# Unread products at the start, later input squares, and a shorter last norm in a two-layer decoder trunk

## The chip, the cores and the metric

The kernel runs on one core of one Trainium2 chip. The metric is the device time of one execution in microseconds (us). Lower is better.

## What is computed

The input is 256 tokens of width 2048, and everything is float32. There are two residual layers. The first has a gated token mixer, the second an attention with forget gates, and each is followed by a feed-forward part with a width-3 causal convolution. Every part begins with an RMS norm, and one more stands at the end. The weights are read once: 417.9 MB. Cut to what matters here:

```
def rmsnorm(x, g):
    r = lax.rsqrt(jnp.mean(x * x, axis=-1, keepdims=True) + EPS)
    return x * r * g

h = x
z = gelu(rmsnorm(h, a_norm) @ a_w_in)          # 2048 -> 4096, halves u and v
h = h + (u * mix(rmsnorm(v, a_v_norm))) @ a_w_out
h = h + conv_ffn(rmsnorm(h, f_norm[0]))        # up 2048 -> 11264, down 5632 -> 2048
h = h + attention(rmsnorm(h, b_norm), keys and values from h)
h = h + conv_ffn(rmsnorm(h, f_norm[1]))        # its down product is the last product of all
return rmsnorm(h, final_norm)
```

## The kernel before

The residual stream `h` lies in SBUF with the feature on the partition: 16 feature tiles of 128, each 256 tokens wide. It is the input, loaded in eight pieces of two tiles (`load_input`), that grows into the output.

**Two parts for every operand.** A product is made to nearly float32 accuracy out of three products in a shorter format. Each weight piece `raw` is split into `whi` (ScalarE, L82) and `wlo`, the rest (VectorE, L83). Each activation tile in the same way: `X[:, kt, :256]` is the rounded part (ScalarE, L221), `X[:, kt, 256:]` the rest (VectorE, L222). TensorE multiplies hi by hi, lo by hi and hi by lo, all on L166.

**The stream.** `Stream` sets the order of all work. Every weight matrix is cut into pieces of 128 x 1024 (512 KB). At step i the program issues the load of piece i + 6 (SyncE queue), the split of piece i + 3, the products of piece i, and then lets every pending generator run up to its next `yield` (`advance`). There are four `raw` buffers and four pairs of `whi` and `wlo`. So a load waits for the split that frees its buffer, and a split waits for the products that free its pair.

**The start.** The first 32 pieces are the v half of `a_w_in`, in four blocks (`tok_block`); activations are the stationary operand there, weights the moving one with 512 columns. A piece of it is 12 products. For the first block each piece also needs its own two tiles of `h`: `input_prep` splits them, has ScalarE square them, and has GpSimd add the squares into `acc` (`square_into_acc(c - 1, nc.gpsimd)`, L266 to L271). The first piece is cut into two halves. I number the pieces of this block 1 to 8.

**Norms.** The scale of each token is applied after the product. `token_sums` sums `acc` over the partitions with TensorE (L244, one moving column of ones, float32) and makes the inverse root on VectorE: a first guess from the bits (L232) and three Newton rounds of three small instructions (L234 to L236). `token_rows` turns the two columns of scales into rows on TensorE (L254). `v_done` reads a v block out of PSUM with Gelu and the scale; a block fills one of three PSUM tiles `ps`.

**The end.** The last down product has eight output blocks of two feature tiles (`feat_block`, 11 pieces each). Weights are stationary. `whi` multiplies 512 columns, the rounded half and the rest of `ffn_H` side by side, and `wlo` multiplies 256, so two halves of `ps` must be added to `h`: L300 and L301 for each tile in `final`. Then follow the squares, for the eighth block (p = 7) the norm, and four multiplications with four output loads (L314, L316).

Of the kernel before, what the change touches and what calls it, by code (L numbers as in the profile page):

```python
# [17 lines left out]
P = 128  # L18
D = 2048
T = 256  # L20
# [112 lines left out]
def build(ctx, tc, d, out):  # L133
# [31 lines left out]
    def mm(o, a, b, start, stop):  # L165
        nc.tensor.matmul(o, a, b, start=start, stop=stop, skip_group_check=True)  # L166

    def feat_block(src, x, K, done):

        box = {}  # L170
        n = K // 4
        for c in range(n):
            def mult(hi, lo, c=c):
                if c == 0:
                    box["ps"] = main_ps()
                ps, xx = box["ps"], x()
                parts = (hi, lo) if c < n - 1 else (lo, hi)
                for i, part in enumerate(parts):
                    for j in range(4):
                        kt = 4 * c + j  # L180
                        for m in range(2):
                            w = part[:, j * 256 + m * P:j * 256 + (m + 1) * P]
                            if part is hi:
                                mm(ps[:, m, :], w, xx[:, kt, :], kt == 0, kt == K - 1)
                            else:
                                mm(ps[:, m, :T], w, xx[:, kt, :T], False, False)
                if c == n - 1:
                    s.start(done(ps))
            s.chunk(src[c], mult)
# [39 lines left out]
    def rsqrt(y, v, n):  # L229

        t = small.tile([P, n], F32, name="rs_t", tag=f"rs_t{n}", bufs=2)
        nc.vector.tensor_scalar(y.bitcast(I32), v.bitcast(I32), -0.5, 1597463007.0, op0=OP.mult, op1=OP.add)  # L232
        for _ in range(3):
            nc.vector.scalar_tensor_tensor(t, y, -0.5, y, op0=OP.mult, op1=OP.mult)  # L234
            nc.vector.tensor_tensor(t, t, v, op=OP.mult)
            nc.vector.scalar_tensor_tensor(y, t, 1.5, y, op0=OP.add, op1=OP.mult)  # L236

    def token_sums(rest=None):

        mp = misc_ps()  # L240
        parts = [acc] + ([] if rest is None else [rest[:, 0, :], rest[:, 1, :]])
        for tb in range(2):
            for i, a in enumerate(parts):
                nc.tensor.matmul(mp[:, tb:tb + 1], a[:, tb * P:(tb + 1) * P], ones[:, :1],  # L244
                                 start=i == 0, stop=i == len(parts) - 1)
        v = small.tile([P, 2], F32, name="ts_v", tag="ts_v", bufs=2)
        nc.vector.tensor_scalar(v, mp[:, :2], 1.0 / D, EPS, op0=OP.mult, op1=OP.add)
        rsqrt(rcol, v, 2)
# [12 lines left out]
        yield  # L261
        nc.scalar.activation(rB, token_rows()[:, :T], AF.Copy)

    def square_into_acc(p, eng=nc.vector):
        sq = small.tile([P, 2, T], F32, name="sq", tag="sq", bufs=2)
        nc.scalar.activation(sq, h[:, 2 * p:2 * p + 2, :], AF.Square)  # L266
        if p == 0:
            eng.tensor_tensor(acc, sq[:, 0, :], sq[:, 1, :], op=OP.add)
        else:
            for i in range(2):  # L270
                eng.tensor_tensor(acc, acc, sq[:, i, :], op=OP.add)  # L271

    def scaled_sum(ps, a):

# [5 lines left out]
    def residual(p, gain):  # L280
# [10 lines left out]
                yield from token_scale()  # L291
        return done

    def final(p, gain):

        def done(ps):
            kts = (2 * p, 2 * p + 1)
            sq = small.tile([P, 2, T], F32, name="sq", tag="sq", bufs=2)
            for m, kt in enumerate(kts):
                nc.vector.tensor_tensor(h[:, kt, :], h[:, kt, :], ps[:, m, :T], op=OP.add)  # L300
                nc.vector.tensor_tensor(h[:, kt, :], h[:, kt, :], ps[:, m, T:], op=OP.add)  # L301
                nc.scalar.activation(sq[:, m, :], h[:, kt, :], AF.Square)
            for kt in kts:
                nc.scalar.activation(h[:, kt, :], h[:, kt, :], AF.Copy, scale=column(gain + kt))
            if p == 0:
                nc.vector.tensor_tensor(acc, sq[:, 0, :], sq[:, 1, :], op=OP.add)
            elif p < 7:
                for i in range(2):
                    nc.vector.tensor_tensor(acc, acc, sq[:, i, :], op=OP.add)
            else:  # L310
                token_sums(sq)
                mp = token_rows()
                for a, b in ((0, 2), (2, 6), (6, 11), (11, 16)):
                    nc.vector.tensor_tensor(h[:, a:b, :], h[:, a:b, :],  # L314
                                            mp[:, None, :T].to_broadcast([P, b - a, T]), op=OP.mult)
                    nc.sync.dma_start(out[:, a:b, :], h[:, a:b, :])  # L316
            yield
        return done
# [37 lines left out]

    def v_done(blk):
        def done(ps):
            _, vt, _, _, ss = mlp_kept()
            for tb in range(2):  # L360
                vv = vt[:, tb, blk * 512:(blk + 1) * 512]
                nc.scalar.activation(vv, ps[:, tb, :], AF.Gelu, scale=rcol[:, tb:tb + 1])
                sq = small.tile([P, 2, T], F32, name="sq", tag="sq", bufs=2)
                nc.scalar.activation(sq.rearrange("p a b -> p (a b)"), vv, AF.Square,
                                     accum_out=ss[:, tb, blk:blk + 1])
# [230 lines left out]
    def g_done(p):  # L596
        def done(ps):
# [4 lines left out]
            while state["done"] < NH or state["gates"] < p:  # L602
# [6 lines left out]
        return done  # L609


    state = {"layer": 0, "heads": [], "done": 0, "gates": 0}
    cd = dram.tile([NH, T], F32, name="cd")

    nc.scalar.dma_start(col[:, :C_KVNORM], d["col"][:, :C_KVNORM])
# [4 lines left out]
    nc.gpsimd.memset(ident, 1.0)  # L620
    nc.gpsimd.affine_select(ident, ident, pattern=[[-1, P]], compare_op=OP.is_equal, fill=0.0,
                            base=0, channel_multiplier=1)
    input_prep(0)

    for blk in range(4):
# [88 lines left out]
```

## Time and profile before

| | before |
|---|---|
| median of 3 runs | 2249.75 us (2249.28 to 2250.73) |
| the profiled execution | 2249.42 us |
| its span, first to last instruction | 2247.7 us |
| TensorE (PE) busy | 2227.7 us, 99% |
| weight load (PEld) | 1920.1 us, 85% |
| VectorE (DVE) | 1530.0 us, 68% |
| ScalarE (ACT) | 1190.9 us, 53% |
| GpSimd (POOL) | 34.7 us, 2% |
| read from HBM | 417.88 MB, 187 GB/s over the span |

The profile covers one execution. Times in its rows are microseconds from the span's start, and a row of the timeline gives start, length, engine, line, operation, output<-inputs and a count; in brackets stands idle time of the engine ahead of it and what ended it. Starts of successive products tell TensorE's pace better than their lengths, since products overlap in the pipeline.

### The profile page before, as it was taken

The numbers are of one execution on the slowest core, as the hardware profiler recorded it, in microseconds if no ns is written. First come the engines' busy times: TensorE is split into PE (matmuls) and PEld (weight loads), VectorE is DVE, ScalarE is ACT, GpSimd is POOL, SyncE is SP. The second block draws the span as 40 slices with busy tenths as digits, with TensorE's granted clock in tenths as the row PEclk, the third lists the DMA queues.
The fourth block names the chain that finished last, engine by engine and source line by source line (L and its number), as shares of the span: only waits on it lengthen the run. The fifth ranks groups of instructions, "written<-read, shape, count | busy, mean of one in ns | idle before, by whom it ended". The sixth has DMA issues, their size and how long they took to land.

```text
span 2247.7 us, 32221 instructions
## 1 busy us (share of the span) xinstructions
PE 2227.7 (99%) x12440; PEld 1920.1 (85%) x12440; DVE 1530.0 (68%) x2212; ACT 1190.9 (53%) x1622; POOL 34.7 (2%) x56
## 2 busy tenths in 40 slices
PE   8999999999999999999999999999999999999997
PEld 6888888888888888888788888888888888888886
DVE  6576677777777755557786567677777777765554
ACT  6544455555555544445444666446555555554442
POOL 3000000000000000000000110000000000000000
PEclk9999999999999999999999999999999999999998
DMA  7565555555555655555555555555555556555553
GB/s 281 186 189 172 191 191 192 189 189 194 190 190 190 191 181 193 197 188 177 171 185 188 167 164 185 181 197 188 189 191 192 189 192 191 190 185 197 189 192 116
DMA packets 116442, 422.11 MB, mean 188 GB/s; under 512 B 13232, under 2 KB 13376, under 8 KB 116032
## 3 DMA queue, kind: packets, MB, share of 16 engines
q1 hardware_dynamic: 115344, 417.93, 56.7%
q0 software_dynamic: 768, 2.10, 0.4%
q8 instruction: 97, 1.59, 0.3%
q14 instruction: 57, 0.47, 0.1%
q10 hardware_dynamic: 176, 0.02, 0.0%
HBM read 417.88 MB, written 2.11 MB: 187 GB/s over the span
## 4 chain that ended last, share of the span: by engine, by line
PE 98%; DVE 1%; ACT 0%; DMA 0%; issue 0%; SPq 0%; DVEq 0%
PE ps L166 96%; PE mp L388 0%; PE mp L472 0%; PE mp L558 0%; DMA raw<-a_in_v 0%; PE mp L573 0%; DVE wlo L83 0%; PE mp L581 0%; PE mp L582 0%; PE mp L557 0%; PE mp L580 0%; DVE X L222 0%; DVE h L314 0%; PE mp L244 0%; ACT whi L82 0%
## 5 line engine op out<-in xcount | busy, mean ns | idle before, releaser
L83 DVE TENSOR_TENSOR wlo<-raw,whi 128x1024 fp32r<-128x1024 f32 (+1 forms) x786 | 954.1, 1222 | 381.5 <-ACT whi L82 380.1
L82 ACT ACTIVATE whi<-raw 128x1024 fp32r<-128x1024 f32 (+1 forms) x786 | 821.8, 1054 | 383.7 <-PE ps L166 346.7
L166 PE MATMUL ps<-X,whi 128*128 128x512 f32 x3328 | 829.6, 396 | 0.0
L166 PEld LDWEIGHTS ps<-X,whi 128*128 128x128 f32 x3328 | 602.3, 188 | 120.7
L166 PEld LDWEIGHTS ps<-X,wlo 128*128 128x128 f32 x3328 | 426.0, 188 | 28.3
L166 PE MATMUL ps<-X,wlo 128*128 128x256 f32 x3328 | 430.7, 277 | 0.0
L166 PE MATMUL ps<-ffn_H,whi 128*128 128x512 f32 x1408 | 354.0, 395 | 0.0
L166 PEld LDWEIGHTS ps<-ffn_H,whi 128*128 128x128 f32 x1408 | 252.7, 188 | 48.5
L276 ACT ACTIVATE half<-ps 128x512 f32<-128x512 f32 x104 | 62.3, 599 | 256.0 <-PE ps L166 256.0
L166 PEld LDWEIGHTS ps<-ffn_H,wlo 128*128 128x128 f32 x1408 | 184.3, 188 | 14.5
L166 PE MATMUL ps<-ffn_H,wlo 128*128 128x256 f32 x1408 | 186.4, 277 | 0.0
L277 DVE TENSOR_TENSOR ffn_a<-ps,half 128x512 f32<-128x512 f32 x88 | 60.9, 692 | 175.3 <-ACT half L276 175.3
L166 PE MATMUL ps<-whi,X 128*128 128x512 f32 x512 | 163.6, 397 | 5.8 <-ACT whi L82 5.8
L166 PE MATMUL ps<-whi,att_X 128*128 128x512 f32 x512 | 168.0, 400 | 0.0
L422 DVE SCALAR_TENSOR_TENSOR ffn_c<-ffn_a,col,ffn_c 128x255 f32<-128x255 f32 x352 | 162.0, 481 | 6.3
L418 ACT ACTIVATE ffn_c<-ffn_a,col 128x256 f32<-128x256 f32 x176 | 96.4, 595 | 47.3 <-DVE ffn_a L278 47.3
L166 PEld LDWEIGHTS ps<-whi,X 128*128 128x128 f32 x512 | 97.0, 189 | 26.3 <-ACT whi L82 5.8
L166 PEld LDWEIGHTS ps<-whi,att_X 128*128 128x128 f32 x512 | 96.2, 188 | 20.5
L166 PE MATMUL ps<-wlo,X 128*128 128x512 f32 x256 | 100.9, 394 | 1.3 <-DVE wlo L83 1.3
L166 PE MATMUL ps<-wlo,att_X 128*128 128x512 f32 x256 | 100.1, 391 | 0.0
L221 ACT ACTIVATE X<-h,col 128x256 fp32r<-128x256 f32 x64 | 29.0, 500 | 101.8 <-DVE h L285 99.5
L226 ACT ACTIVATE ffn_H<-ffn_c 128x256 fp32r<-128x256 f32 x88 | 36.8, 418 | 70.0 <-DVE ffn_c L426 70.0
(140 smaller groups left out, 1223.4 us busy)
## 6 DMA issues: line engine op xcount, KB each, us to landing
raw<-up SPq DMA_DIRECT2D x352, 512.0 KB, 3.7
raw<-down SPq DMA_DIRECT2D x176, 512.0 KB, 3.9
raw<-a_in_u SPq DMA_DIRECT2D x32, 512.0 KB, 3.5
raw<-a_out SPq DMA_DIRECT2D x32, 512.0 KB, 3.9
raw<-b_q SPq DMA_DIRECT2D x32, 512.0 KB, 4.2
raw<-kvf_k SPq DMA_DIRECT2D x32, 512.0 KB, 3.5
raw<-kvf_v SPq DMA_DIRECT2D x32, 512.0 KB, 3.8
raw<-b_g SPq DMA_DIRECT2D x32, 512.0 KB, 3.3
```

What stands on the lines that cost most here:

```text
L82: self.nc.scalar.activation(hi[:, :n], raw, AF.Copy)
L83: self.nc.vector.tensor_tensor(lo[:, :n], raw, hi[:, :n].bitcast(F32), op=OP.subtract)
L166: nc.tensor.matmul(o, a, b, start=start, stop=stop, skip_group_check=True)
L221: nc.scalar.activation(dst[:, kt, :T], h[:, kt, :], AF.Copy, scale=g)
L226: nc.scalar.activation(dst[..., :T], src, AF.Copy)
L276: nc.scalar.activation(t, ps[:, :, T:], AF.Copy)
L277: nc.vector.tensor_tensor(a, ps[:, :, :T], t, op=OP.add)
L418: nc.scalar.activation(c[:, m, :], a[:, m, :], AF.Identity, scale=w[2], bias=column(C_CONVB + l * 2 * KF + f))
L422: nc.vector.scalar_tensor_tensor(c[:, m, n:], a[:, m, :T - n], w[k], c[:, m, n:], op0=OP.mult, op1=OP.add)
```

## The change

It has four parts.

1. `warm_up(9)`: nine 128 x 128 float32 products of the identity with itself into a PSUM tile that nobody reads, ahead of the first real product.
2. The squares of the input leave GpSimd. `input_prep` no longer squares; `input_norm` waits three steps and then squares one pair of tiles in each of eight steps, ScalarE squaring and VectorE adding. The sums, the scales and `rB` come after that, and `v_done` waits until `state["normed"]` is set.
3. In the last output block (`last_block`, p = 7) each feature tile gets its own run of 12 products of 256 columns in each piece, all into one 256-column half of `ps`. So one addition to `h` is enough for a tile, and tile 14 is added and squared while the products of tile 15 run (`final_tile`). The sums of `acc` go ahead of the products of tile 15 in the last piece.
4. In the last norm ScalarE takes the square root, VectorE its reciprocal, and one Newton round follows instead of a guess and three. A tiny Sqrt at p = 5 brings the table load forward.

```diff
+    def last_block(src, x, K, done, last):
...
+                for m in range(2):
+                    for part, half in ((lo, 0), (hi, 1), (hi, 0)):
+                        for j in range(4):
+                            kt = 4 * c + j
+                            mm(ps[:, m, :T], part[:, j * 256 + m * P:j * 256 + (m + 1) * P],
+                               xx[:, kt, half * T:(half + 1) * T], part is lo and kt == 0,
+                               half == 0 and part is hi and kt == K - 1)
+                    if c == n - 1:
+                        last(ps, m)
...
+    def newton(y, v, t):
+        nc.vector.scalar_tensor_tensor(t, y, -0.5, y, op0=OP.mult, op1=OP.mult)
+        nc.vector.tensor_tensor(t, t, v, op=OP.mult)
+        nc.vector.scalar_tensor_tensor(y, t, 1.5, y, op0=OP.add, op1=OP.mult)
...
+    def final_tile(ps, m):
+
+        kt = KD - 2 + m
+        if m == 0:
+            tail["sums"] = misc_ps()
+            tail["sq"] = small.tile([P, 2, T], F32, name="sq", tag="sq", bufs=2)
+            sum_tokens(tail["sums"], acc, True, False)
+        nc.vector.tensor_tensor(h[:, kt, :], h[:, kt, :], ps[:, m, :T], op=OP.add)
+        nc.scalar.activation(tail["sq"][:, m, :], h[:, kt, :], AF.Square)
+
+    def sum_tokens(mp, a, first, last):
+        for tb in range(2):
+            nc.tensor.matmul(mp[:, tb:tb + 1], a[:, tb * P:(tb + 1) * P], ones[:, :1],
+                             start=first and tb == 0, stop=last and tb == 1, skip_group_check=True)
...
             for kt in kts:
                 nc.scalar.activation(h[:, kt, :], h[:, kt, :], AF.Copy, scale=column(gain + kt))
...
-                token_sums(sq)
+            if p == 5:
+                nc.scalar.activation(warm, ones, AF.Sqrt)
+            if p == 7:
+                for m in range(2):
+                    sum_tokens(tail["sums"], tail["sq"][:, m, :], False, m == 1)
+                v = small.tile([P, 2], F32, name="ts_v", tag="ts_v", bufs=2)
+                nc.vector.tensor_scalar(v, tail["sums"][:, :2], 1.0 / D, EPS, op0=OP.mult, op1=OP.add)
+                t = small.tile([P, 2], F32, name="rs_t", tag="rs_t2", bufs=2)
+                nc.scalar.activation(t, v, AF.Sqrt)
+                nc.vector.reciprocal(rcol, t)
+                newton(rcol, v, t)
                 mp = token_rows()
...
     def input_prep(c):
         for kt in (2 * c, 2 * c + 1):
             prep(X1, kt, C_ANORM)
-        if c >= 1:
-            square_into_acc(c - 1, nc.gpsimd)
         if c == 7:
             s.start(input_norm())
 
+    def warm_up(n):
+
+        mp = misc_ps()
+        for _ in range(n):
+            nc.tensor.matmul(mp[:, :P], ident, ident, start=True, stop=True)
+
     def input_norm():
-        square_into_acc(7, nc.gpsimd)
-        yield
+        for _ in range(3):
+            yield
+        for p in range(8):
+            yield
+            square_into_acc(p)
         yield
         token_sums()
         yield
         nc.scalar.activation(rB, token_rows()[:, :T], AF.Copy)
+        state["normed"] = True
...
     def v_done(blk):
         def done(ps):
+            while not state["normed"]:
+                yield
...
-            feat_block(d[f"down{l}"][11 * p:11 * p + 11], ffn_h, KF, done(p))
+            feat_block(d[f"down{l}"][11 * p:11 * p + 11], ffn_h, KF, done(p), final_tile if l and p == 7 else None)
...
+    warm_up(9)
     input_prep(0)
```

How it moves instructions is seen at three places. Each row is a line of the program, an operation, output<-inputs, the shape and a count; line numbers are those of the kernel that the rows belong to. The first place is VectorE (DVE) at the start, from piece 7 of the first block on; `X_73` is the split input, `wlo` a weight piece's rest, `acc` the sum of squares. Before:

```order
L83 TENSOR_TENSOR wlo<-raw,whi 128x1024
L222 SCALAR_TENSOR_TENSOR X_73<-h,col,X_73 128x256 x2
L83 TENSOR_TENSOR wlo<-raw,whi 128x1024 x2
L247 TENSOR_SCALAR ts_v<-mp 128x2
L232 TENSOR_SCALAR rcol<-ts_v 128x2
```

After, at the same place on VectorE:

```order
L83 TENSOR_TENSOR wlo<-raw,whi 128x1024
L246 SCALAR_TENSOR_TENSOR X_73<-h,col,X_73 128x256 x2
L83 TENSOR_TENSOR wlo<-raw,whi 128x1024 x5
L291 TENSOR_TENSOR acc<-sq 128x256
L83 TENSOR_TENSOR wlo<-raw,whi 128x1024
L294 TENSOR_TENSOR acc<-acc,sq 128x256 x2
```

The additions, which stood on GpSimd, now lie between the weight splits of the second and third block, two to a piece; ahead of them VectorE's order in the first block is what it was.

The second place is TensorE (PE) at the end of the program; `sq` holds the squares of the last two tiles. Before:

```order
L166 MATMUL ps<-ffn_H,wlo 128x256 x16
L166 MATMUL ps<-ffn_H,whi 128x512 x8
L244 MATMUL mp<-ones,acc 128x1
L244 MATMUL mp<-ones,sq 128x1 x2
L244 MATMUL mp<-ones,acc 128x1
L244 MATMUL mp<-ones,sq 128x1 x2
L254 MATMUL mp<-ident,rcol 128x128 x2
```

After, TensorE's last rows:

```order
L166 MATMUL ps<-ffn_H,wlo 128x256 x4
L166 MATMUL ps<-ffn_H,whi 128x256 x8
L329 MATMUL mp<-ones,acc 128x1 x2
L166 MATMUL ps<-ffn_H,wlo 128x256 x4
L166 MATMUL ps<-ffn_H,whi 128x256 x8
L329 MATMUL mp<-ones,sq 128x1 x4
L277 MATMUL mp<-ident,rcol 128x128 x2
```

The two sums of `acc` have moved into the last piece, and the four sums of `sq` are alone behind it, the first two of them over tile 14.

The third place is VectorE at the end, from the last weight split on. Before, up to the end of the first Newton round (L234 to L236 come twice more, and then L314):

```order
L83 TENSOR_TENSOR wlo<-raw,whi 128x1024 x8
L300 TENSOR_TENSOR h<-h,ps 128x256
L301 TENSOR_TENSOR h<-h,ps 128x256
L300 TENSOR_TENSOR h<-h,ps 128x256
L301 TENSOR_TENSOR h<-h,ps 128x256
L247 TENSOR_SCALAR ts_v<-mp 128x2
L232 TENSOR_SCALAR rcol<-ts_v 128x2
L234 SCALAR_TENSOR_TENSOR rs_t<-rcol 128x2
L235 TENSOR_TENSOR rs_t<-rs_t,ts_v 128x2
L236 SCALAR_TENSOR_TENSOR rcol<-rs_t,rcol 128x2
```

After, up to the first output multiplication:

```order
L83 TENSOR_TENSOR wlo<-raw,whi 128x1024 x8
L324 TENSOR_TENSOR h<-h,ps 128x256 x2
L355 TENSOR_SCALAR ts_v<-mp 128x2
L358 RECIPROCAL rcol<-rs_t 128x2
L261 SCALAR_TENSOR_TENSOR rs_t<-rcol 128x2
L262 TENSOR_TENSOR rs_t<-rs_t,ts_v 128x2
L263 SCALAR_TENSOR_TENSOR rcol<-rs_t,rcol 128x2
L362 TENSOR_TENSOR h<-h,mp 128x512
```

Two of four additions are gone, and of ten small instructions between `ts_v` and the scales four are left, with a square root of ScalarE between `ts_v` and the reciprocal.

More of the change, by code (lines that the diff above doesn't have):

```diff
@@ L166, in mm, with feat_block @@
         nc.tensor.matmul(o, a, b, start=start, stop=stop, skip_group_check=True)
-    def feat_block(src, x, K, done):
+    def feat_block(src, x, K, done, last=None):
+        if last:
+            return last_block(src, x, K, done, last)
         box = {}
@@ L186, in mult @@
                                 mm(ps[:, m, :T], w, xx[:, kt, :T], False, False)
+                if c == n - 1:
+                    s.start(done(ps))
+            s.chunk(src[c], mult)
+    def last_block(src, x, K, done, last):
+        box = {}
+        n = K // 4
+        for c in range(n):
+            def mult(hi, lo, c=c):
+                if c == 0:
+                    box["ps"] = main_ps()
+                ps, xx = box["ps"], x()
+                for m in range(2):
[5 more added lines that the diff above has]
+                               half == 0 and part is hi and kt == K - 1)
+                    if c == n - 1:
+                        last(ps, m)
                 if c == n - 1:
@@ L233, in rsqrt, with token_sums @@
         for _ in range(3):
[L234 to L238, printed above, removed]
-        mp = misc_ps()
[L241 to L245, printed above, removed]
+            newton(y, v, t)
+    def newton(y, v, t):
+        nc.vector.scalar_tensor_tensor(t, y, -0.5, y, op0=OP.mult, op1=OP.mult)
+        nc.vector.tensor_tensor(t, t, v, op=OP.mult)
+        nc.vector.scalar_tensor_tensor(y, t, 1.5, y, op0=OP.add, op1=OP.mult)
+    def token_sums():
+        mp = misc_ps()
+        sum_tokens(mp, acc, True, True)
         v = small.tile([P, 2], F32, name="ts_v", tag="ts_v", bufs=2)
@@ L267, in square_into_acc @@
         if p == 0:
[L268 removed]
+            nc.vector.tensor_tensor(acc, sq[:, 0, :], sq[:, 1, :], op=OP.add)
         else:
             for i in range(2):
[L271 removed]
+                nc.vector.tensor_tensor(acc, acc, sq[:, i, :], op=OP.add)
     def scaled_sum(ps, a):
@@ L609, in g_done @@
         return done
-    state = {"layer": 0, "heads": [], "done": 0, "gates": 0}
+    tail = {}
+    state = {"normed": False, "layer": 0, "heads": [], "done": 0, "gates": 0}
     cd = dram.tile([NH, T], F32, name="cd")
```

24 lines of the change are left out of this document (12 added, 12 removed).

## Prediction

> **What bounds the kernel now.** I read the page first, then busy time by stretches, to see whether TensorE ever waits in the body:
>
> ```profile
> 33.00:2231.90 2198.90, 2198.90 (x12327) 1898.71 (x12325) 1495.86 (x2156) 1167.06 (x1581) 18.36 (x34) 1.00 0.57 187
> ```
>
> The first figure behind the stretch is its length, the second TensorE's busy time, and they are equal: from 33 us to the last product TensorE never waits. What ends earlier ahead of 33 us therefore moves the whole body, as does work behind 2231.9 us. Only those ends have something to give. TensorE's timeline at the start:
>
> ```profile
> 5.77 0.79 PE L166 MATMUL ps<-whi,X 128*128 128x512 f32 x1 [5.77 <-ACT whi L82]
> ...
> 7.09 1.05 PE L166 MATMUL ps<-whi,X 128*128 128x512 f32 x2
> ...
> 10.23 0.62 PE L166 MATMUL ps<-whi,X 128*128 128x512 f32 x2
> 10.79 0.50 PE L166 MATMUL ps<-wlo,X 128*128 128x512 f32 x1
> ...
> 27.01 0.50 PE L166 MATMUL ps<-wlo,X 128*128 128x512 f32 x1 [0.42 <-DVE wlo L83]
> ...
> 28.50 0.39 PE L166 MATMUL ps<-wlo,X 128*128 128x512 f32 x1
> ...
> 29.19 0.39 PE L166 MATMUL ps<-wlo,X 128*128 128x512 f32 x1
> ...
> 29.65 0.50 PE L244 MATMUL mp<-ones,acc 128*128 128x1 f32 x4
> 30.01 0.48 PE L166 MATMUL ps<-whi,X 128*128 128x512 f32 x1
> ```
>
> Two things. Two products take 1.05 at 7.09 and 0.62 at 10.23. The fast pair, with 0.39 for its second product, makes a new one every 0.23 us; the slow pair, drawn out alike, one every 0.4. TensorE begins at about half pace, though the profile's clock column doesn't tell so there. And a piece needs 12 products: three take 29.19 - 28.50 = 0.69, so twelve 2.76. But from the `wlo` of piece 2 (10.79) to that of piece 7 (27.01) five pieces took 16.22 instead of 13.80. The bracket names VectorE's `wlo` as what ended the wait. VectorE's and GpSimd's rows say why it is late:
>
> ```profile
> 7.91 0.48 DVE L222 SCALAR_TENSOR_TENSOR X<-h,col,X 128x256 fp32r<-128x256 f32 x1
> 9.51 1.23 DVE L83 TENSOR_TENSOR wlo<-raw,whi 128x1024 fp32r<-128x1024 f32 x1 [1.12 <-ACT whi L82]
> ...
> 19.98 1.84 DVE L222 SCALAR_TENSOR_TENSOR X<-h,col,X 128x256 fp32r<-128x256 f32 x2
> 21.74 1.77 DVE L83 TENSOR_TENSOR wlo<-raw,whi 128x1024 fp32r<-128x1024 f32 x1
> ...
> 15.48 12.07 POOL L271 TENSOR_TENSOR acc<-acc,sq 128x256 f32<-128x256 f32 x10 [0.30 <-ACT sq L266]
> ```
>
> While GpSimd adds squares, two X rests take 1.84 instead of twice 0.48 and a `wlo` 1.77 instead of 1.23. That is 3.5 us a piece, more than TensorE's 2.76. Alone it is about 2.15.
>
> **The change part by part.** The sum is made against the profiled execution: 2249.42 us, 1.72 of it outside the span of 2247.7. The median, 2249.75, lies 0.33 above it, and I put the result against the median.
>
> *Unread products: 0.* They wait for `ident` and stand ahead of the first real product on TensorE:
>
> ```profile
> 1.12 0.29 POOL L621 TENSOR_SCALAR_AFFINE_SELECT ident<-ident 128x128 f32<-128x128 f32 x1
> ```
>
> A float32 product leaves two records (the two sums at 29.65 left four, about 0.11 apart at full clock, so about 0.21 at half). Nine make 18 records, 3.9 us from 1.4 on: done at 5.3, ahead of 5.77. If each took a whole cold length, 0.35, they would end at 7.7, piece 1 at 10.5. With the clock up, piece 1 ends near 6.50 + 11 x 0.23 = 9.0 instead of 10.46, where the second product of the pair at 10.23 starts, piece 2's first. But then it waits, because this chain does not move:
>
> ```profile
> 2.66 0.43 SPq L70 DMA_DIRECT2D raw<-a_in_v  x1
> ...
> raw<-a_in_v SPq DMA_DIRECT2D x1, 512.0 KB, 5.7
> ...
> 8.42 1.06 ACT L82 ACTIVATE whi<-raw 128x1024 fp32r<-128x1024 f32 x1
> ...
> 10.71 1.04 ACT L82 ACTIVATE whi<-raw 128x1024 fp32r<-128x1024 f32 x1
> ```
>
> Piece 2's load is issued at 2.66 and lands 5.7 later, at 8.4. ScalarE splits at once, VectorE follows at 9.51 to 10.74, undisturbed already, and TensorE has its `wlo` at 10.79. So the 1.4 us won become idle time. Bounds: 0 to -0.3 (a restart of 0.1 or so, no more), nothing lost while the nine end ahead of 7.7.
>
> *Squares off GpSimd: -2.4.* From 10.79 on I expect pieces of 2.76, so 16.22 - 13.80 = 2.4 comes back. What is late next? Piece 3: its `whi` was done at 11.75 even before; VectorE goes on at 10.74 with two X rests (0.96) and `wlo` (1.23), done at 12.9; TensorE wants it at 10.79 + 2.76 = 13.55. Spare 0.6, and each later piece gains 0.6 more. Bounds: half if something else ends the waits (rival below), all of it if not.
>
> *Squares and norm later: 0.* For ScalarE's part I take the rows of the v blocks' readout:
>
> ```profile
> L362 ACT ACTIVATE mlp_vt<-ps,rcol 128x512 f32<-128x512 f32 x8 | 5.4, 678 | 6.0 <-PE ps L166 6.0
> L364 ACT ACTIVATE sq<-mlp_vt 128x512 f32<-128x512 f32 x8 | 5.1, 633 | 0.4
> ```
>
> In eight steps VectorE gets a `wlo` of 1.23 and two additions of a quarter of its width, each under half of its time: below 2.5 us in a piece of 2.76. ScalarE gets 1.06 and a square of 512 columns like L364, 0.63. Neither falls behind. The new wait in `v_done` holds two PSUM tiles; the third block uses the third, and the fourth needs the first back. By the order of steps the norm is done in the second piece of the third block, so some six pieces, 16 us, remain. Then two blocks are read at once, on ScalarE four pairs of 0.68 + 0.63, 5.2 us, in two pieces that leave it 2 x (2.76 - 1.06) = 3.4. Queued behind are weight splits, which run three pieces (8.3 us) ahead. That lead covers the 1.8; without it, 1.8 would be lost. The sums themselves cost TensorE as much as before.
>
> *Last block in 256 columns: -0.5; sums of `acc` inside it: +0.4.*
>
> ```profile
> 2228.31 1.98 PE L166 MATMUL ps<-ffn_H,wlo 128*128 128x256 f32 x16
> 2230.12 2.02 PE L166 MATMUL ps<-ffn_H,whi 128*128 128x512 f32 x8
> 2231.99 0.28 PE L244 MATMUL mp<-ones,acc 128*128 128x1 f32 x2
> ```
>
> 16 products of 256 columns, each with its own weight load, took 1.81 (0.1135 each); 8 of 512 took 1.87 (0.233). A piece goes from 8 x (0.1135 + 0.233) = 2.77 to 24 x 0.1135 = 2.72; eleven give -0.5. Bounds -0.6 and 0. The sums of `acc` now cut into the last piece. At 29.19 the same sums stretched two product steps, 0.46, to 30.01 - 29.19 = 0.82; with a slow restart +0.4, bounds 0.3 and 0.5. They cost nothing before, as the squares ended later.
>
> *The tail: -3.0, and -0.2 for the clock.* The chain that ended last:
>
> ```profile
> 2232.19 0.43 DVE h L300
> ...
> 2232.64 0.42 DVE h L301
> ...
> 2233.88 0.42 ACT sq L302
> ...
> 2234.35 1.40 PE mp L244 x8
> ...
> 2235.78 0.17 DVE ts_v L247
> ...
> 2235.97 0.18 DVE rcol L232
> ...
> 2237.96 0.70 PE mp L254 x2
> ...
> 2238.69 0.69 DVE h L314
> ```
>
> From the first addition to the row transposes it took 2237.96 - 2232.19 = 5.77. The new chain, step by step: one addition 0.45 (2232.19 to 2232.64), the square 0.47 (2233.88 to 2234.35), four records of sums 0.65 (eight took 1.40), `ts_v` 0.20 (2235.78 to 2235.97). Then the root, a reciprocal and one Newton round:
>
> ```profile
> L619 ACT ACTIVATE warm<-ones 128x2 f32<-128x2 f32 x1 | 0.2, 203 | 0.0
> ...
> L566 DVE RECIPROCAL att_sm<-att_sm 128x2 f32<-128x2 f32 x16 | 2.7, 166 | 13.6 <-ACT att_big L565 13.6
> ...
> 2234.21 0.89 ACT L304 ACTIVATE h<-h,col 128x256 f32<-128x256 f32 x2
> ```
>
> The root as a tiny ScalarE step 0.23, the reciprocal 0.20, three small VectorE steps of 0.20. In all 2.80, so 3.0 less. The root queues behind two scalings of `h`; they started 0.33 after the last square and took 0.89, so they end 1.67 into the chain and `ts_v` at 1.77: covered by 0.1. The table load at p = 5 falls where ScalarE is half idle. The two sums over tile 14 fit between the last product and the last square. Bounds for the chain: 2.5 to 3.2.
>
> The windows of the tail show the clock (the 1.00 and 0.50 ahead of the last two figures):
>
> ```profile
> 2232.50:2234.90 2.40, 0.93 (x7) 0.85 (x7) 1.28 (x4) 1.43 (x4) 0.00 (x0) 1.00 0.00 0
> 2234.90:2239.00 4.10, 1.53 (x7) 1.04 (x6) 2.09 (x12) 0.20 (x1) 0.00 (x0) 0.50 0.00 0
> ```
>
> The transposes ran at half clock, 0.73 to the first multiplication. Three microseconds earlier they probably run at full clock: two float32 steps of 0.11 less each, -0.2, bounds 0 and -0.3.
>
> Sum: 0 - 2.4 + 0 - 0.5 + 0.4 - 3.0 - 0.2 = -5.7: 2249.42 becomes 2243.7, and the median 2244.05. I forecast **2244.0 us**. The measurement can tell 0.2%, 4.5 us, from no change: the edge is 2245.25.
>
> **The rivals.** *The clock falls again* (0.12). The idle time that I expect between 9.0 and 10.79 is new. For it: the tail's clock fell although TensorE was busy 0.93 of 2.40 us ahead of that. Against it: TensorE would be busy over half of any such stretch. At the start the clock rose between the slow pair at 7.09 and the fast one at 10.23, some 3 us after the first product; so long at half pace, 7 products come instead of 13 or 14, and 6.5 of 0.23 are +1.5: 2245.6. The Trainium skill ("TensorE: Matmul & The Clock Gate", Part 1) says that the gate judges free-running windows of about 3.4 us and halves the clock after an idle one; by it nothing would fall here, as no gap is that long. The trace does not quite agree: the fall at 2234.9 followed a stretch that was not idle.
>
> *Another supplier is late in the first block* (0.13). The loads are close:
>
> ```profile
> 10.79:13.75 2.96, 2.96 (x13) 2.18 (x12) 2.96 (x4) 2.96 (x6) 2.13 (x3) 1.00 1.04 413
> ```
>
> At 10.79 to 13.75 the queues were full at 413 GB/s. Pieces of 768 KB every 2.76 us ask for 285, so I expect no wait; if half the 2.4 stays, 2245.2.
>
> *Slower: weight loads show* (0.05). The last block loads each `whi` twice, 24 loads a piece instead of 16.
>
> ```profile
> L166 PEld LDWEIGHTS ps<-ffn_H,wlo 128*128 128x128 f32 x1408 | 184.3, 188 | 14.5
> ```
>
> If a load showed its whole 0.188 us, 264 products would cost 264 x (0.188 - 0.1135) = 20 more: 2264. From 0.135 a product on, the change loses. Against it stand the 16 `wlo` products in a row, each with a load, at 0.1135. The Trainium skill (same page, "LDWEIGHTS") puts a load of 128 columns at 128 / 1.2 = 107 ns, an estimate under the trace's pace.
>
> That the unread products do nothing is in the forecast already.
>
> **How the numbers follow.** Forecast 0.70, clock 0.12, supplier 0.13, weight loads 0.05. Faster by over 0.2%: nearly all of the forecast (0.68) and half of the supplier's case, 0.74. Same: clock 0.12, the other half, a rest of 0.02: 0.20. Slower: 0.06, with 0.01 for what I don't see. The range takes the forecast's bounds below (-0.1 last block, -0.2 chain, -0.3 start, some 0.5 that the runs spread under the median) to 2242.8, and above the clock and supplier cases with some spread, to 2246.3. Outside are the weight loads and what is left of the ends.
>
> **What would show it.** Right: the first `wlo` product of piece 2 still near 10.79, with TensorE idle ahead of it; then 2.76 a piece and no wait on `wlo`; VectorE's X rests at 0.48 and `wlo` at 1.23 up to 27; eleven last pieces of 2.72; first addition to transposes about 2.8, clock 1.00 there. Wrong: products 0.43 apart behind 10.8, waits for ScalarE or a load at pieces 3 to 8, a TensorE gap at the fourth block's start, 0.13 or more between the last block's products, or a second table load in the tail.

## The result and the profile after

| | before | after |
|---|---|---|
| median | 2249.83 us | 2244.39 us |
| lowest and highest of 11 runs | 2249.23 to 2250.78 | 2244.03 to 2244.74 |
| the profiled execution | 2249.42 | 2244.26 |
| its span | 2247.7 | 2242.6 |

The ratio of after to before is 0.9975, with a 95% interval of 0.9968 to 0.9983: 5.44 us less, 0.24%. The forecast was 2244.0 in a range of 2242.8 to 2246.3, so the number was right. Two of its steps were not. The sums of `acc` cost twice what was forecast, and the reason given for the unread products does not hold in every execution. By the profiled pair, -5.7 was forecast and -5.1 came.

The body first, busy time by stretches as in the prediction (length, TensorE, weight loads, VectorE, ScalarE, GpSimd, granted clock):

```profile
33.00:2229.90 2196.90, 2196.73 (x12410) 1901.68 (x12409) 1501.45 (x2180) 1170.78 (x1589) 18.47 (x34) 1.00 0.57 186
```

Here 0.17 us are missing from TensorE's busy time, where before none was. They will turn up at the end of the last block. TensorE's timeline of the start:

```profile
1.46 3.98 PE L382 MATMUL mp<-ident 128*128 128x128 f32 x18 [1.46 <-POOL ident L680]
6.04 0.50 PE L166 MATMUL ps<-whi,X 128*128 128x512 f32 x1 [0.59 <-ACT whi L82]
...
9.19 0.40 PE L166 MATMUL ps<-whi,X 128*128 128x512 f32 x1
9.88 0.50 PE L166 MATMUL ps<-whi,X 128*128 128x512 f32 x1 [0.30 <-ACT whi L82]
11.14 0.50 PE L166 MATMUL ps<-wlo,X 128*128 128x512 f32 x1 [0.76 <-DVE wlo L83]
...
27.73 0.39 PE L166 MATMUL ps<-wlo,X 128*128 128x512 f32 x1
```

The eighteen records of the unread products end at 5.44, ahead of the first real product. That one now takes 0.50 instead of 0.79: the clock is already up. Piece 1 is through at about 9.4, and TensorE then idles for `whi` and `wlo` of piece 2, as expected; the `wlo` comes at 11.14 instead of 10.79. From there to the `wlo` of piece 8 six pieces take 16.59, or 2.765 each, without a wait. The first five take 13.84, where before they took 16.22. The reason stands in VectorE's timeline:

```profile
18.94 0.88 DVE L246 SCALAR_TENSOR_TENSOR X<-h,col,X 128x256 fp32r<-128x256 f32 x2
19.75 1.23 DVE L83 TENSOR_TENSOR wlo<-raw,whi 128x1024 fp32r<-128x1024 f32 x1
```

Two X rests 0.88 instead of 1.84, a `wlo` 1.23 instead of 1.77: GpSimd no longer adds beside them. The end, in TensorE's timeline:

```profile
2227.93 0.50 PE L329 MATMUL mp<-ones,acc 128*128 128x1 f32 x4
2228.61 0.74 PE L166 MATMUL ps<-ffn_H,wlo 128*128 128x256 f32 x4 [0.17 <-DVE h L324]
2229.18 1.07 PE L166 MATMUL ps<-ffn_H,whi 128*128 128x256 f32 x8
2230.09 0.50 PE L329 MATMUL mp<-ones,sq 128*128 128x1 f32 x4
```

Between the sums of `acc` and the products of tile 15 stands a wait that the prediction did not have. Its releaser is VectorE's addition of tile 14. The chain that ended last tells the same and then the short tail:

```profile
2228.13 0.43 DVE h L324
...
2228.61 1.66 PE ps L166 x12
...
2230.29 0.43 DVE h L324
...
2230.74 0.42 ACT sq L325
...
2231.21 0.62 PE mp L329 x4
...
2231.85 0.17 DVE ts_v L355
...
2232.05 0.21 ACT rs_t L357
...
2233.09 0.45 PE mp L277 x2
...
2233.56 0.69 DVE h L362
```

From the last addition to the transposes 2233.09 - 2230.29 = 2.80, where it was 5.77 from the first of four additions. The transposes take 0.47 to the first multiplication instead of 0.73, at full clock (the 0.99 below comes from the fall at 2233.97, behind them):

```profile
2232.00:2234.00 2.00, 0.43 (x2) 0.19 (x2) 1.10 (x6) 0.20 (x1) 0.00 (x0) 0.99 0.00 0
```

### The profile page after: what moved, and what is told of

Read it like the earlier page. It is cut to its first block, busy times and chain, and to the rows that moved or that the text cites. A ratio compares the mean times of both kernels' runs of the same rounds, so it can differ in the third digit from the quotient of the medians.

```text
span 2242.6 us, 32429 instructions
## 1 busy us (share of the span) xinstructions
PE 2228.1 (99%) x12546; PEld 1927.1 (86%) x12546; DVE 1528.5 (68%) x2219; ACT 1193.5 (53%) x1625; POOL 19.2 (1%) x41
## 3 DMA queue, kind: packets, MB, share of 16 engines
HBM read 417.88 MB, written 2.11 MB: 187 GB/s over the span
## 4 chain that ended last, share of the span: by engine, by line
PE 99%; DVE 0%; DMA 0%; ACT 0%; SPq 0%; DVEq 0%; issue 0%
PE ps L166 97%; PE mp L446 0%; PE mp L530 0%; PE mp L616 0%; DMA raw<-a_in_v 0%; PE mp L631 0%; PE mp L639 0%; PE mp L640 0%; PE mp L615 0%; PE mp L638 0%; DVE h L362 0%; PE mp L329 0%; PE mp L277 0%; DVE wlo L83 0%; DVEq L768 0%; ACT whi L82 0%
## 5 line engine op out<-in xcount | busy, mean ns | idle before, releaser
L166 PE MATMUL ps<-ffn_H,whi 128*128 128x512 f32 (+1 forms) x1496 | 355.4, 381 | 0.0
L166 PEld LDWEIGHTS ps<-ffn_H,whi 128*128 128x128 f32 x1496 | 258.7, 188 | 45.3
```

## The experiments

The theory going in was the prediction's: GpSimd's additions slow VectorE at the start (-2.4), the short chain ends the kernel earlier (-3.0), and the unread products do nothing. The rivals were that the unread products matter after all, and that what hurt at the start was not GpSimd beside VectorE but something else that the change also moved. Times are medians; "before" is the kernel before in the same runs. Its medians, 2249.61 to 2249.89, differ by 0.28 between the sets of runs, so a difference of a few tenths between kernels of different sets shows little by itself.

### Without the unread products

```diff
-    warm_up(9)
```

> The changed kernel without its nine unread products. As predicted they are worth nothing, because the wlo of piece 2 sets TensorE's start on piece 2: 2244.4 us, within 0.3 of the changed kernel. Rival: now that VectorE no longer holds pieces 2 to 8 back, products at half pace behind piece 2 are paid in full, and how long they last depends on when the clock rises: 2244.4 to 2245.2, runs more spread than the 0.7 us of the changed kernel, and in the trace products 0.43 us apart behind the first wlo of piece 2.

Measured: 2244.96 (2243.94 to 2245.77) against 2249.78, ratio 0.9979 (0.997 to 0.9987). That is 0.57 more than the changed kernel, and a spread of 1.83 instead of 0.71. The two intervals overlap, so the medians alone would not carry this; TensorE's timeline shows where it comes from:

```profile
6.17 0.79 PE L166 MATMUL ps<-whi,X 128*128 128x512 f32 x1 [6.17 <-ACT whi L82]
...
10.04 1.05 PE L166 MATMUL ps<-whi,X 128*128 128x512 f32 x2
10.90 0.63 PE L166 MATMUL ps<-wlo,X 128*128 128x512 f32 x1
11.32 0.70 PE L166 MATMUL ps<-whi,X 128*128 128x512 f32 x2
11.86 0.40 PE L166 MATMUL ps<-wlo,X 128*128 128x512 f32 x1
```

Products stand 0.43 apart up to 11.32; the trace's clock record rises at 11.46. In this execution piece 1 ended so late that no idle time was left ahead of piece 2: VectorE had the first `wlo` of piece 2 ready at 11.10, and TensorE took it at 11.86, where in the changed kernel it was ready at 11.09 and taken at 11.14. So the half clock cost 0.72 here. This execution is the slowest of the eleven, 1.51 above the profiled one of the changed kernel, and the half clock is only part of that: from piece 2 to piece 17 it then took 42.00 instead of 41.31, 2.80 a piece instead of 2.75, at full clock (see the last section). The lowest run, 2243.94, is level with the lowest with unread products, 2244.03. The other profiles agree: in the eight with unread products TensorE took this `wlo` 0.05 or 0.06 after it was ready, in the six without them 0.05 to 1.01 after. So the half clock costs between nothing and about 1 us by when it ends, and the unread products take that out. That they gain 0.57 in the median fits this, but is not shown clear of the noise.

### The unread products alone

To the kernel before, `warm_up(9)` is added and nothing else.

> The kernel before with the nine unread products alone (part 1 of the change). Theory: there VectorE is late for pieces 3 to 7 whatever TensorE's pace, so an early clock is worth nothing: 2249.8, with the spread of the kernel before. Rival: an early clock is worth the 0.6 us that it is worth in the changed kernel: 2249.2.

Measured: 2250.06 (2249.11 to 2250.83) against 2249.61, ratio 1.0001 (0.9992 to 1.0009). Nothing gained, nothing lost. Its profile has the `wlo` of piece 2 at 10.82, that of piece 8 at 30.37 and the next matrix at 99.06, where before had 10.79, 30.32 and 99.02: VectorE sets the pace through piece 8, and TensorE's start does not matter. Only once VectorE is out of the way can the same edit be worth the 0.57 of the experiment before.

### The squares alone

To the kernel before, part 2 of the change: no squares in `input_prep`, the later `input_norm`, the wait in `v_done`.

> The kernel before with the squares and the norm moved alone (part 2 of the change). Theory: VectorE's splits are back at 1.23 us and TensorE runs pieces 2 to 8 at 2.76 us each: 2.4 us less than before, 2247.4. Rival, another supplier ends the waits: half of it, 2248.6. If half pace at the start is paid now, up to 0.8 of the gain is missing.

Measured: 2247.91 (2246.69 to 2248.11) against 2249.78, ratio 0.999 (0.9981 to 0.9999): -1.87. Its profile has pieces 2 to 8 from 11.57 to 28.05, 2.75 each, without a wait for `wlo`, so the 2.4 is there; its first `wlo` of piece 2 is 0.78 later than before's. TensorE took it at 11.57, though VectorE had it ready at 10.97: the first product came 0.70 later than before's, and the clock rose at 10.48 instead of 9.41. The gain and this loss add up to -1.6, near the median's -1.87.

### Squares at their old place, added by VectorE

To the kernel before:

```diff
-            square_into_acc(c - 1, nc.gpsimd)
+            square_into_acc(c - 1)
...
-        square_into_acc(7, nc.gpsimd)
+        square_into_acc(7)
```

> The kernel before with the squares' additions on VectorE instead of GpSimd, at their old place in the first block. If it is GpSimd's disturbance alone that makes VectorE late, most of the 1.9 us of the squares alone comes back: 2248.0. If VectorE's own load decides too (two X rests 0.88, wlo 1.23 and two additions 0.85 make 2.96 a piece against TensorE's 2.76), about a third to a half of it: 2249.

Measured: 2248.36 (2247.68 to 2249.09) against 2249.89, ratio 0.9994 (0.9985 to 1.0003): -1.53 in the medians, though the interval just reaches 1. VectorE's timeline:

```profile
16.92 0.88 DVE L222 SCALAR_TENSOR_TENSOR X<-h,col,X 128x256 fp32r<-128x256 f32 x2
17.71 0.88 DVE L271 TENSOR_TENSOR acc<-acc,sq 128x256 f32<-128x256 f32 x2
18.51 1.22 DVE L83 TENSOR_TENSOR wlo<-raw,whi 128x1024 fp32r<-128x1024 f32 x1
```

Here VectorE does more work, the two additions as well, and is faster: 2.73 a piece instead of 3.5, and no product waits for `wlo`. (The expectation's 2.96 a piece added lengths that overlap; by starts it is 2.73.) So it was GpSimd beside VectorE that cost the time, not the amount of work. What the later place adds is room: 2.73 is just under TensorE's 2.76, and the sums of `acc` at the end of the block still waited for the last addition, a gap of 1.05 us between starts at 27.79 and 28.84.

### Squares later, but added by GpSimd

To the changed kernel:

```diff
-            square_into_acc(p)
+            square_into_acc(p, nc.gpsimd)
```

> The changed kernel with the additions of the squares on GpSimd again, but still late, in the second and third block. If what mattered is that VectorE is disturbed while it is the limit, it costs nothing here, since VectorE has a wlo of 1.2 to 1.8 us to make in a piece of 2.76: 2244.4. Rival, GpSimd's additions slow VectorE's splits enough wherever they stand: some of the 2.4 us comes back, 2245 to 2247.

Measured: 2246.20 (2245.76 to 2250.22) against 2249.61, ratio 0.999 (0.9981 to 0.9998): 1.8 slower than the change. It was expected to cost nothing. The rival's 2245 to 2247 holds the median, but the way was another one. VectorE's splits were slowed again (two `wlo` took 4.64 us at 40.30), yet no product waited for one, since splits run three pieces ahead by then. GpSimd's timeline shows what did it, and after it stand TensorE's, and then two stretches of the windows:

```profile
40.17 2.00 POOL L410 TENSOR_SCALAR_AFFINE_SELECT mlp_wT<-mlp_wT 128x2048 f32<-128x2048 f32 x1 [2.70 <-DMA mlp_wT<-wsT]
42.15 15.33 POOL L294 TENSOR_TENSOR acc<-acc,sq 128x256 f32<-128x256 f32 x12
```

```profile
57.53 0.79 PE L329 MATMUL mp<-ones,acc 128*128 128x1 f32 x4 [1.88 <-POOL acc L294]
...
59.18 1.05 PE L166 MATMUL ps<-whi,X 128*128 128x512 f32 x2
```

```profile
54.41:57.82 3.41, 1.53 (x9) 0.98 (x7) 2.49 (x2) 1.56 (x2) 2.99 (x2) 1.00 0.56 177
57.82:61.23 3.41, 3.41 (x10) 2.82 (x11) 2.52 (x12) 0.00 (x0) 0.00 (x0) 0.50 0.50 168
```

The additions were queued behind GpSimd's mask of `mlp_wT`, which waited for its load. So the sums of `acc` came too late by 1.88 us, TensorE stood still, and then the clock fell to half for 3.41 us. The eleven times lie in two groups, 2245.76 to 2246.20 and 2247.68 to 2250.22; the profiled execution, 2248.54, is of the upper one. The lower group is 1.4 to 1.8 above the change, about the wait alone; the upper one fits a wait with a fallen clock behind it, though only the one profile shows it.

### The end alone

To the kernel before, parts 3 and 4 of the change.

> The kernel before with the last block and the last norm alone (parts 3 and 4). Theory from the two traces: last block 0.6 less, sums of acc with the wait behind them 0.8 more, chain 3.0 less, clock 0.25 less: 3.0 less than before, 2246.8. Rival: the end's gain rests on the clock's phase and vanishes in part in other runs: 2247.1.

Measured: 2246.65 (2246.17 to 2246.85) against 2249.78, ratio 0.9986 (0.9977 to 0.9994): -3.13. Its chain from the addition at 2232.34 to the transposes at 2235.14 takes 2.80, and its last block 30.89, the same as in the changed kernel. With the -1.87 of the squares alone and the 0.57 of the unread products this gives -5.57, against -5.44 for all of it.

### The short root alone

To the kernel before, part 4: the root on ScalarE, one Newton round, the tiny Sqrt at p = 5.

> The kernel before with the new norm alone (part 4): root on ScalarE, reciprocal, one Newton round. Theory: ten small VectorE steps of 0.196 (1.97 us) become root, reciprocal and three steps, 1.04: 0.9 less than before, 2248.8; the other 2.1 of the end's gain then belongs to part 3. Rival: the clock decides more than the steps and the gain is 0.6 or 1.2.

Measured: 2248.64 (2248.0 to 2249.27) against 2249.89, ratio 0.9994 (0.9985 to 1.0003): -1.25, and the interval reaches 1. The chain carries it: 4.50 from the first addition at 2232.40 to the transposes, instead of 5.77. From `ts_v` on it takes 1.24 instead of 2.18:

```profile
2235.66 0.17 DVE ts_v L247
...
2235.85 0.21 ACT rs_t L250
...
2236.90 0.70 PE mp L262 x2
```

The 0.94 is the root. Another 0.33 is not: in this execution the eight records of sums ran at full clock and took 1.07 instead of 1.40. So of the 3.0 the root gives about 0.9. That leaves about 2.0 for the order of the last block, which takes additions and sums out of the chain; part 3 was not run by itself.

### Two PSUM tiles for the last block

The wait at 2228.61 suggests that the products of tile 15 are held because they go to the same PSUM tile `ps` that VectorE is reading. To the changed kernel:

```diff
-                    box["ps"] = main_ps()
+                    box["ps"] = [main_ps(), main_ps()]
...
+                    ps = box["ps"][m]
```

> The changed kernel with the last block's two tiles in two PSUM tiles, so that the products of tile 15 need not wait for VectorE's addition of tile 14. Theory: the 0.4 us gap behind the sums of acc goes, 0.3 to 0.4 less than the changed kernel, 2244.0. Rival: the gap is a restart behind float32 products and stays: 2244.4.

Measured: 2244.18 (2243.87 to 2244.34) against 2249.78, ratio 0.9976 (0.9966 to 0.9986). The median is 0.21 lower, too little for the intervals, but the chain of one execution shows the step gone: the products of tile 15 follow the sums at once, and the last block takes 30.59 instead of 30.89.

```profile
2227.96 0.34 PE mp L330 x4
2228.30 1.53 PE ps L166 x12
2229.86 0.43 DVE h L325
```

### The sums of the older squares moved behind the products

In addition to the two tiles, the sums of `acc` go behind the products of tile 15, where TensorE waits for the last square anyway:

```diff
     def final_tile(ps, m):
...
-            sum_tokens(tail["sums"], acc, True, False)
...
             if p == 7:
+                sum_tokens(tail["sums"], acc, True, False)
                 for m in range(2):
```

> The changed kernel with two PSUM tiles in the last block and the sums of acc behind its products, in the time in which TensorE waits for the last square. Theory: the wait (0.3) and the sums' own 0.45 go, 0.7 less than the changed kernel, 2243.7. Rival: eight records of sums no longer fit ahead of the last square and the chain grows by what they stick out: 2244.0.

Measured: 2243.76 (2243.3 to 2244.31) against 2249.61, ratio 0.9974 (0.9964 to 0.9984), on the expected value. The last block takes 30.09, 0.80 less than in the changed kernel: 0.30 the wait and 0.50 the sums. TensorE's timeline shows the eight records of sums where it was idle:

```profile
2229.32 0.50 PE L329 MATMUL mp<-ones,acc 128*128 128x1 f32 x4
2229.68 0.58 PE L329 MATMUL mp<-ones,sq 128*128 128x1 f32 x4
2230.44 0.61 PE L329 MATMUL mp<-ones,sq 128*128 128x1 f32 x4 [0.17 <-ACT sq L325]
2232.32 0.69 PE L278 MATMUL mp<-ident,rcol 128*128 128x128 f32 x2 [1.28 <-DVE rcol L264]
```

In this execution the clock fell at 2231.72, so the transposes took 0.73 again.

### All weight-stationary products in 256 columns

In the last block two products of 256 columns cost less than one of 512. The same split, then, in every block in which weights are stationary:

```diff
-                                mm(ps[:, m, :], w, xx[:, kt, :], kt == 0, kt == K - 1)
+                                mm(ps[:, m, :T], w, xx[:, kt, :T], kt == 0, kt == K - 1)
+                                mm(ps[:, m, T:], w, xx[:, kt, T:], False, kt == K - 1)
```

> The changed kernel with every whi product of all other weight-stationary blocks made as two products of 256 columns with a weight load each, as in the last block. If the pace of the last block (24 products of 0.1133 us, 2.72 a piece, against 2.7735) holds everywhere, 645 pieces save 0.05 each: some 33 us less, 2211. Rival: the gain is peculiar to the last block, or the weight loads, then without a gap, begin to wait: 2244 or above.

Measured, in five runs: 2266.99 (2266.39 to 2268.45) against 2249.61, ratio 1.008 (1.0066 to 1.0093). 2211 was expected, and this is 22.6 more than the change. In the first up product TensorE's timeline has

```profile
399.77 0.28 PE L166 MATMUL ps<-X,whi 128*128 128x256 f32 x1
399.89 2.05 PE L166 MATMUL ps<-X,wlo 128*128 128x256 f32 x16
401.78 2.40 PE L166 MATMUL ps<-X,whi 128*128 128x256 f32 x19
```

Sixteen starts in 1.89 us, 0.118 each. The up and down products and the last block ran at that pace; the u half, `a_out`, `b_out` and part of the gate at 0.113. The last block's products are those of the changed kernel, yet it took 32.0 instead of 30.89. So the pace is not a property of the shape: the same run of products has two.

### 256 columns where they ran fast, on top of the best end

The two tiles and the later sums, and the split only in the u half of `a_w_in`, `a_out`, the gate and `b_out`; the up and down blocks keep 512 columns.

> The changed kernel with two PSUM tiles and the sums of acc behind the products of the last block, and with whi products of 256 columns in the u, a_out, gate and b_out blocks only, not in up and down. If the pace of 0.1133 us that those blocks had when all blocks were cut holds without the others, they save 1.7, 1.8 and 2.7 us and the last block 0.6: 2237.5. Rival: the slow pace of 0.118 moves to these blocks: 2246.

Measured, in five runs: 2237.52 (2236.85 to 2239.64) against 2249.89, ratio 0.9946 (0.9933 to 0.9958), on the expected value: 12.4 below the kernel before and 6.9 below the change. It beats both. Its timeline in `a_out`:

```profile
203.34 1.07 PE L166 MATMUL ps<-mlp_X,wlo 128*128 128x256 f32 x8
204.25 1.98 PE L166 MATMUL ps<-mlp_X,whi 128*128 128x256 f32 x16
206.06 1.07 PE L166 MATMUL ps<-mlp_X,wlo 128*128 128x256 f32 x8
```

24 starts in 2.72 us, 0.1133 each. The u half alone went from 95.1 to 93.4.

### The token blocks in 256 columns too

On top of that, the products of `tok_block`, with activations stationary, are cut into halves of 256 columns.

> The kernel of c1_best with the products of the token-stationary blocks (v, q, keys, values) cut to 256 columns as well. If their pace goes from 0.230 for 512 columns to 0.1133 for 256, 128 pieces save 0.04 each, 5 us less than c1_best. Rival: they fall to the slow pace, 0.118, 128 pieces lose 0.07 each, 9 us more than c1_best, and in the first block the clock or VectorE decide anyway.

Measured: 2250.75 (2245.02 to 2252.27) against 2249.89, ratio 1.0 (0.9991 to 1.0009): 13.2 worse than without it, as the rival had it and more. The profiled execution is the slowest of the eleven. The u half, which is not touched by this edit, went back from 93.4 to 96.7, the pace of 0.118. The last block kept 30.09. The eleven times lie 7 us apart, so the pace may differ between executions of one kernel as well; only one was profiled. What chooses it is open: no run here tells the loads of weights, the fetching of instructions and a phase between them apart.

This kernel's profile shows one thing more, the prediction's rival of the falling clock at its own place. The windows of its start, each one step of the clock's grid (see the last section):

```profile
8.27:11.68 3.41, 1.76 (x13) 1.35 (x12) 1.67 (x3) 2.68 (x4) 0.00 (x0) 1.00 1.03 390
11.68:15.09 3.41, 3.41 (x18) 3.41 (x18) 3.41 (x5) 3.16 (x7) 0.00 (x0) 0.50 0.98 387
```

The first holds the idle time ahead of piece 2, TensorE is busy 1.76 of it, and the next step runs at half clock. The changed kernel's own window there:

```profile
8.48:11.90 3.42, 2.36 (x9) 1.43 (x8) 2.04 (x5) 3.01 (x5) 0.00 (x0) 1.00 1.04 412
```

Busy 2.36, and the clock stayed up.

## Why the prediction was right, by its own steps

By the two profiled executions the span fell by 5.1 us. The prediction's terms, each with what the traces have:

| step | expected | found | from |
|---|---|---|---|
| unread products | 0 | 0 in this pair; 0.57 of the median, not clear of the noise | first two experiments |
| start of piece 2 (part of the same step) | 10.79 | 11.14: +0.35 | timeline |
| squares off GpSimd | -2.4 | -2.4 | 16.22 to 13.84 |
| squares and norm later | 0 | 0 | no TensorE wait after 11.14 up to 2228 |
| last block in 256 columns | -0.5 | -0.6 | 30.67 to 30.09, the latter with the sums moved out |
| sums of `acc` inside it | +0.4 | +0.8 | last block 30.09 to 30.89 |
| the chain | -3.0 | -3.0 | 5.77 to 2.80 |
| clock at the transposes | -0.2 | -0.3 | 0.73 to 0.47 |

The found terms add up to -5.1, as the span does. The sums and the start of piece 2 miss in the same direction, by 0.4 and 0.35, and the last block and the clock give back 0.1 each.

**Squares off GpSimd** was right in size and reason. That VectorE and not something else set the pace is shown by both sides: additions on VectorE at the old place take the waits away though it works more, and the unread products alone bring nothing.

**The chain** came out step by step, with the root covered as the prediction had it: `ts_v` ends at 2232.02 and the root starts at 2232.05.

**The sums of `acc`** is a term that was mis-sized, at +0.4 for +0.8. The prediction counted four sums that cut into the products. It missed that the products of tile 15 write into the other half of the PSUM tile that VectorE reads for tile 14, and so wait for it: 0.30 by the experiment with two tiles. The sums themselves are 0.50, at the bound that was given. The text of the change had it in view (all products go into one `ps`, an addition stands between its two halves), and the sentence "tile 14 is added and squared while the products of tile 15 run" was taken at its word.

**The last block** came out at -0.6 for -0.5 because of a division: the prediction's row has 16 products in 1.81, which is 0.1131 each and not 0.1135, and with that the same sum gives -0.66.

**Unread products: 0** is the step whose reason failed. The idle time expected ahead of piece 2 is there with unread products. But the prediction took the time at which the clock rises in the kernel before, between 7.09 and 10.23, as given; the clock records say 9.41 for that execution. In the six profiles without unread products it rose at 9.41, 10.04, 10.48, 10.99, 11.08 and 11.46; the late ones outlast the wait for piece 2, and where VectorE does not hold the next pieces back nothing gives that time back. The kernel before that was profiled had the earliest rise of the six, so that the forecast of 0 fits this pair is partly luck. In the eight with them it rose between 4.60 and 7.62, but for one (10.03, the kernel with GpSimd's late additions). The Trainium skill ("TensorE: Matmul & The Clock Gate", Part 1) says of this that the windows are free-running, so that the same kernel sees the change at different times. The trace agrees: the stretch at full clock lasted 2228.90 us in the changed kernel and 2225.49 or 2222.08 in others, which are 653, 652 and 651 times 3.4133 us.

**The start of piece 2** was right but for its load: 6.1 us from issue to landing instead of 5.7.

```profile
raw<-a_in_v SPq DMA_DIRECT2D x1, 512.0 KB, 6.1
```

The load scatters without unread products as well: in the six profiles without them it landed at 8.19 to 9.13, in the eight with them at 8.20 to 9.35. So the traces give no reason to put it down to the extra products.

**The clock at the transposes** was a bet with a poor reason. "Three microseconds earlier" does not decide it; the grid of 3.41 us does. In the changed kernel the clock fell at 2233.97, 0.4 behind the transposes' end; with the sums moved, the end came earlier still, and yet it fell ahead of them, at 2231.72.

Of the rivals, the falling clock and the late supplier did not happen in the changed kernel: all products of the first block stand at full pace, with no wait after 11.14. The reason given against the first, that TensorE is busy over half of any such stretch, is not enough: at 2.36 of 3.42 the clock stayed up, but at 1.76 of 3.41, also just over half, it fell. The margin was some 0.6 us of idle time at most. Weight loads that show did not happen in the last block, at 2.72 a piece. But the price at which they would was nearer than the prediction thought: at 0.118 a product instead of 0.1133 the same block costs 1.1 more, as the kernel with all weight-stationary products in 256 columns shows.

## What to carry to other kernels

When an engine is late, look first at what runs beside it and not at how much it has to do: VectorE with more work and a quiet GpSimd was faster than with less work and a busy one. A wait that bounds a stage hides every other edit there, so an edit that measures nothing alone (the unread products) may gain something beside the one that removes the bound. And where a step is said to overlap another, look at which buffer each of them holds; a PSUM tile that is shared by halves is one buffer to the wait.

## What the runs showed of the hardware that was not expected

The clock of TensorE changes on a grid of 3.413 us (the two half-clock stretches ahead of the tail lasted just that long), and a step of it need not be idle for the clock to fall. Ahead of the tail it fell after the two steps with 1.76 busy (the first block) and 1.53 (the kernel with GpSimd's late additions); in the first blocks it stayed after steps with 2.36 and more. The Trainium skill ("TensorE: Matmul & The Clock Gate", Part 1) has the fall after an idle window. By these numbers a window about half busy is enough. In the tail it is less simple: it stayed after 2.11 (squares added early by VectorE) and 2.23 (unread products alone), but fell after 2.21 (token blocks in 256 columns) and, with the sums moved, after 2.56. The last two steps hold all twelve records of the sums, whose products have one column. What the gate counts as busy is not settled here.

A row of products of 256 columns, each with its own load of 128 x 128 weights, has two paces, 0.1133 and 0.118 us, that hold over long stretches. The same split made a kernel 22.6 us slower where the slow pace came with it and 6.2 faster where it did not (2243.76 to 2237.52). Products of 512 columns can do the same: in the profiled execution without unread products, pieces 2 to 16 took 2.80 each, 0.2333 a product, and from piece 20 on 2.75, or 0.229. With the token blocks in 256 columns the pace went from 2.83 a piece to 2.72 at the same place. Between, in pieces 17 to 19, the sums and the transposes of the first norm cut into the row of products. That suggests that an interruption can change the pace; no run here tests it. The cause is open.
